# A quarter's y in three parts: dense products and the next quarter's kernel of lags traced between them

## The chip, the cores and the metric

One core of a Trainium2 chip runs the whole kernel. The metric is the device time of one execution in microseconds (us), the median of several runs. TensorE is PE in the profile, VectorE DVE, ScalarE ACT, GpSimd POOL, and SP is the queue that issues most DMAs.

## The reference, cut to what matters

One layer of a hybrid encoder over 1024 frames of 1024 channels, in float32:

```
u = rmsnorm(h);  proj = u @ w_in            # u_ssm | q | k | v
y_ssm  = S5 state space model(u_ssm)        # x_t = A x_{t-1} + B u_t ; y = Re(C x) + D u ; gelu ; GLU
y_attn = stick-breaking attention(q, k, v)  # 8 heads of 64
g_ssm, g_attn = sigmoid(u @ w_gate + b)
h = h + (g_ssm * (y_ssm @ w_up_ssm) + g_attn * (y_attn @ w_up_attn)) @ w_out
h = h + relu(rmsnorm(h) @ W1)^2 @ W2 ;  out = rmsnorm(h)
```

The change is in the part that forms y and its gelu in the state space model, and in how products of `u @ w_in` and `u @ w_gate` lie between its pieces.

## The kernel before, in words

The frames are cut into 128 blocks of 8. The states at the blocks' borders come from a tree of prefix sums on VectorE (`prefix_sums`). Then `ssm_y(q)` (L677) forms y for a quarter of the channels, q = 0 to 3, in three steps:

1. The kernel of lags: two loads on SP (L679: `cst[q]` to tag "h", `xq[q]` to tag "t"), a second "t" tile `tq`, eight 128x128 matmuls L686 into two "tr" banks of PSUM, and two copies L688 on ScalarE into `tq`.
2. y itself: the matmuls L700 to L702 into two "tr" banks (from `x`, `tq`, the states and `c`), two copies L703 into an "e" tile, and the gelu as a chain of four: square L705 on ScalarE, L706 on VectorE (in the trace under its helper's line, L145), sigmoid L707 on ScalarE, product L708 on VectorE (L142, e<-e,q).
3. The turn: eight transposes L714 into two "tr" banks, two copies L715 into a tile of tag "a", and its store to DRAM (L716, issued by SP at L76).

Each matmul of 128x128 float32 is two records in the trace, so L686 has 16 a quarter and L700, L701 and L702 have 16 each.

Beside this runs `fill`, a generator over the dense products (the projections of q, k, v and the gates, in pairs of weight blocks, seven products to a pair). An item has operands and a product. The operands (L604) are at most two sums, then a copy L620 on ScalarE to the high part and a subtraction L621 on POOL (in the trace L142, a<-a,a or a<-raw,a) to the low part, both in a new "a" tile. The product (L624) is 12 matmuls of 128x512 (L149, L152, L155) into one of the two "mm" banks. `pipelined(..., 2)` traces the operands of an item two items ahead of its product. The loop at L729 traces all of `ssm_y(q)` and then four steps of `fill` (BESIDE_Y), four times. After it comes the attention: its first steps turn v (L757, "tr" banks) and form scores (L779), and its weights go to "e" tiles in memory that the "e" and "four" tiles of this stage gave up (L835).

The order in which each engine runs its instructions isn't written by hand. It is fixed when the program is built: what is traced earlier goes first among what a timing model there holds to be ready. Tiles of a tag are given out in the order of tracing; a tile that is not free yet makes its first writer wait. The tags that matter: "tr" has 2 banks, "mm" 2, "t" 2 tiles, "a" 24 (of which the split activations `uT` hold 16 and their differences 2).

Of the kernel before, what the change touches and what calls it, by code (L numbers as in the profile page):

```python
# [31 lines left out]
BESIDE_Y = 4  # L32
# [21 lines left out]
def layer_kernel(ctx: ExitStack, tc: tile.TileContext, a, out):  # L54
# [17 lines left out]
    def stored(x, queue):  # L72

        count[0] += 1
        d = dp.tile([P, 1024], F32, tag=f"dram{count[0]}", name=f"dram{count[0]}")
        queue.dma_start(d, x)  # L76
        return d

    def load(src, tag):
        x = slot(tag)  # L80
        nc.sync.dma_start(x, src)
        return x

    def slot(tag, dtype=F32, cols=1024):
        count[0] += 1
        pool, bufs = beside.get(tag) or (sb, SLOTS[tag])
        return pool.tile([P, cols], dtype, tag=tag, bufs=bufs, name=f"{tag}{count[0]}")
# [11 lines left out]
    def bank(tag, dtype=F32):  # L99
        count[0] += 1  # L100
        return pp.tile([P, 512], dtype, tag=tag, bufs=BANKS[tag], name=f"{tag}{count[0]}")
# [39 lines left out]
    def tt(o, x, y, op, eng=None):  # L141
        (eng or V).tensor_tensor(o, x, y, op=op)  # L142

    def stt(o, x, s, y, op0, op1):
        V.scalar_tensor_tensor(o, x, s, y, op0=op0, op1=op1)  # L145
# [170 lines left out]
    with tc.issue_after(last_norm[0].ins):  # L316
# [19 lines left out]
        def exp_parts(x):  # L336

            xc = small()
            ts(xc, x, -88.0, ALU.max, 89.0, ALU.min)
            n = rounded(xc, 1.4426950408889634)  # L340
            r = small()
            stt(r, n, -0.693359375, xc, ALU.mult, ALU.add)
            stt(r, n, 2.12194440054690583e-4, r, ALU.mult, ALU.add)
            e = horner(r, [1.0 / math.factorial(i) for i in range(1, 10)])
            ni = small()
            nv = ni.bitcast(I32)
            ts(n, n, 127.0, ALU.add, 0.0, ALU.max)
            ts(n, n, 8388608.0, ALU.mult)
            V.tensor_copy(nv, n)
            pw = ni  # L350
            ex, em = small(), small()
            stt(ex, e, 1.0, pw, ALU.add, ALU.mult)
            tt(em, e, pw, ALU.mult)
            ts(r, pw, -1.0, ALU.add)
            tt(em, em, r, ALU.add)
            return ex, em

        dt, _ = exp_parts(ldt)
# [223 lines left out]
    def pipelined(items, ahead):  # L582

        for i in range(len(items) + ahead):
            if i < len(items):
                items[i][0]()
            if i >= ahead:
                items[i - ahead][1]()
                yield
# [87 lines left out]
    def ssm_y(q):  # L677

        c, x, tq = load(cst[q], "h"), load(xq[q], "t"), slot("t")  # L679

        tv = tq.rearrange("p (g t c) -> p t g c", g=8, t=L)
        for tb in range(2):
            ps = bank("tr")
            for i in range(4):
                t = tb * 4 + i
                PE.matmul(ps[:, i * P:(i + 1) * P], lhsT=iflat[:, (7 - t) * 16:(7 - t) * 16 + P],  # L686
                          rhs=kc[:, 512 + q * P:512 + (q + 1) * P], start=True, stop=True)
            S.activation(tv[:, tb * 4:tb * 4 + 4], ps.rearrange("p (t g c) -> p t g c", t=4, g=8), AF.Copy)  # L688
        y = slot("e")
        yv = y.rearrange("p (t g c) -> p g t c", t=L, g=8)  # L690
        tv = tq.rearrange("p (g x) -> p g x", g=8)
        cv = c.rearrange("p (g r x) -> p g r x", g=4, r=2)
        sv = sq[q]
        for e in range(2):
            ps = bank("tr")
            rows = slice(e * 64, e * 64 + 64)
            for i in range(4):
                g = 2 * i + e
                o = ps[:, i * P:(i + 1) * P]
                PE.matmul(o, lhsT=x[:, g * P:(g + 1) * P], rhs=tv[:, g], start=True, stop=False)  # L700
                PE.matmul(o, lhsT=sv[rows, 0, g // 2], rhs=cv[rows, g // 2, 0], start=False, stop=False)  # L701
                PE.matmul(o, lhsT=sv[rows, 1, g // 2], rhs=cv[rows, g // 2, 1], start=False, stop=True)  # L702
            S.activation(yv[:, e::2], ps.rearrange("p (g t c) -> p g t c", g=4, t=L), AF.Copy)  # L703
        w = slot("q")
        S.activation(w, y, AF.Square)  # L705
        stt(w, w, 1.0 / 0.044715, y, ALU.add, ALU.mult)  # L706
        S.activation(w, w, AF.Sigmoid, scale=2.0 * math.sqrt(2.0 / math.pi) * 0.044715)  # L707
        tt(y, y, w, ALU.mult)  # L708
        r = slot("a")
        rv = r.rearrange("p (k t) -> p t k", t=L)  # L710
        for th in range(2):
            ps = bank("tr")
            for i in range(4):
                PE.transpose(ps[:, i * P:(i + 1) * P], y[:, (th * 4 + i) * P:(th * 4 + i + 1) * P], ident)  # L714
            S.activation(rv[:, th * 4:th * 4 + 4], ps.rearrange("p (t k) -> p t k", t=4), AF.Copy)  # L715
        yT.append(stored(r, nc.sync))  # L716

    rest = [(j, p) for p in range(1, 4) for j in range(3)] + [("g", m) for m in GATES[PLAIN:]]
    fill = pipelined([x for i in range(0, len(rest), 2) for x in projected(rest[i:i + 2])], 2)
# [6 lines left out]
            next(sums, None)  # L726
    for _ in sums:
        pass
    for q in range(4):  # L729
        ssm_y(q)  # L730
        for _ in range(BESIDE_Y):
            next(fill)

    def split(x, tag):
# [625 lines left out]
```

## Time and profile before

| | us |
|---|---|
| median of 3 runs | 1528.75 |
| the three runs | 1527.75, 1528.75, 1528.93 |
| the profiled execution's own time | 1536.21 |
| its span, first to last instruction | 1534.1 |
| PE busy in the span | 1421.0 (93%) |
| mean granted clock of TensorE | 0.964 |

The profiled execution has its own time; around the span lie 2.11 us. A line of the timeline gives the start and the duration of an instruction or of a merged run of them (x10: ten), its engine and line, what it writes and reads, and in brackets how long the engine stood idle before it and what released it. [...]

### The profile page before, as it was taken

The numbers are of one execution on the slowest core, as the hardware profiler recorded it, in microseconds if no ns is written. First come the engines' busy times: TensorE is split into PE (matmuls) and PEld (weight loads), VectorE is DVE, ScalarE is ACT, GpSimd is POOL, SyncE is SP. The second block draws the span as 40 slices with busy tenths as digits, with TensorE's granted clock in tenths as the row PEclk, the third lists the DMA queues.
The fourth block names the chain that finished last, engine by engine and source line by source line (L and its number), as shares of the span: only waits on it lengthen the run. The fifth ranks groups of instructions, "written<-read, shape, count | busy, mean of one in ns | idle before, by whom it ended". The sixth has DMA issues, their size and how long they took to land.

```text
span 1534.1 us, 18436 instructions
## 1 busy us (share of the span) xinstructions
PE 1421.0 (93%) x6858; PEld 1123.2 (73%) x6858; DVE 1095.9 (71%) x1477; ACT 596.2 (39%) x1061; POOL 787.5 (51%) x448
## 2 busy tenths in 40 slices
PE   6999677998999899999999899999999899999786
PEld 6898556765666566678888678888887688887565
DVE  7996993128676767752734986655557999999997
ACT  5315112245555555641332633333332533333324
POOL 4102663134443333421240557777777788887963
PEclk9999799899999999999999999999999899999988
DMA  6113113232221211445421033333327433331002
GB/s 227 70 43 136 55 56 124 69 124 82 71 81 69 83 42 69 157 140 176 164 77 55 1 123 116 118 110 110 110 83 280 149 111 113 114 99 55 0 28 110
DMA packets 43432, 153.53 MB, mean 100 GB/s; under 512 B 5072, under 2 KB 5072, under 8 KB 43344
## 3 DMA queue, kind: packets, MB, share of 16 engines
q1 hardware_dynamic: 38448, 135.31, 26.1%
q10 hardware_dynamic: 4896, 17.06, 2.8%
q8 instruction: 54, 0.88, 0.2%
q14 instruction: 34, 0.28, 0.1%
HBM read 108.83 MB, written 43.52 MB: 99 GB/s over the span
## 4 chain that ended last, share of the span: by engine, by line
PE 36%; DVE 21%; issue 2%; POOL 1%; ACT 1%; DMA 1%; DVEq 0%; POOLq 0%; ACTq 0%
DVE a L142 5%; PE z L155 5%; PE z L152 5%; PE z L149 5%; DVE w L1149 5%; PE mm L149 4%; PE mm L152 4%; PE mm L155 3%; DVE h L142 3%; DVE raw L142 3%; PE tr L155 2%; PE tr L149 2%; PE tr L152 2%; DVE e L142 1%; DVE t L142 1%
## 5 line engine op out<-in xcount | busy, mean ns | idle before, releaser
L142 POOL TENSOR_TENSOR a<-raw,a 128x512 fp32r<-128x512 f32 (+2 forms) x70 | 99.1, 1424 | 245.3 <-ACT a L620 200.8
L149 PE MATMUL mm<-a,a 128*128 128x512 f32 (+1 forms) x369 | 147.0, 401 | 9.1 <-DVE a L142 6.9
L155 PE MATMUL mm<-a,a 128*128 128x512 f32 (+1 forms) x369 | 143.2, 389 | 1.9 <-DVE a L142 1.8
L152 PE MATMUL mm<-a,a 128*128 128x512 f32 (+1 forms) x369 | 144.4, 392 | 0.0
L790 DVE TENSOR_TENSOR_SCAN e<-e 128x512 f32<-128x512 f32 (+3 forms) x96 | 111.8, 1174 | 44.2 <-ACT e L785 44.1
L142 POOL TENSOR_TENSOR a<-a,a 128x512 fp32r<-128x512 f32 x36 | 53.3, 1481 | 122.4 <-ACT a L620 122.1
L142 POOL TENSOR_TENSOR a<-e,a 128x512 fp32r<-128x512 f32 (+1 forms) x71 | 107.8, 1530 | 10.7 <-ACT a L1038 9.8
L1038 ACT ACTIVATE a<-e 128x512 fp32r<-128x512 f32 x84 | 52.6, 631 | 137.9 <-POOL e L142 37.1
L142 DVE TENSOR_TENSOR a<-mm,a 128x512 f32<-128x512 f32 x96 | 65.2, 681 | 57.2 <-PE mm L155 52.8
L149 PEld LDWEIGHTS mm<-a,a 128*128 128x128 f32 x369 | 71.5, 195 | 25.0 <-issue 8.1
L155 PEld LDWEIGHTS mm<-a,a 128*128 128x128 f32 x369 | 71.3, 193 | 16.8 <-DVE a L142 2.2
L152 PEld LDWEIGHTS mm<-a,a 128*128 128x128 f32 x369 | 71.8, 195 | 13.3 <-DVE a L257 0.3
L142 DVE TENSOR_TENSOR a<-a,a 128x512 f32<-128x512 f32 (+2 forms) x52 | 58.6, 1131 | 30.5 <-ACT a L620 10.3
L132 POOL TENSOR_TENSOR w<-raw,w 128x1024 fp32r<-128x1024 f32 x13 | 33.3, 2564 | 82.3 <-ACT w L131 82.3
L1149 POOL TENSOR_TENSOR e<-a,e 128x1024 fp32r<-128x1024 f32 (+1 forms) x24 | 73.8, 3079 | 2.7 <-ACT e L1148 2.7
L1149 POOL TENSOR_TENSOR e<-raw,e 128x1024 fp32r<-128x1024 f32 x21 | 56.0, 2669 | 25.9 <-ACT e L1148 25.9
L152 PE MATMUL z<-e,w 128*128 128x512 f32 x156 | 63.3, 406 | 6.0 <-POOL e L1149 6.0
L155 PE MATMUL mm<-w,a 128*128 128x512 f32 x158 | 67.3, 426 | 0.0
L152 PE MATMUL mm<-w,a 128*128 128x512 f32 x158 | 67.2, 425 | 0.0
L142 DVE TENSOR_TENSOR e<-e,e 128x256 f32<-128x256 f32 (+4 forms) x81 | 62.7, 784 | 4.9
L149 PE MATMUL mm<-w,a 128*128 128x512 f32 x158 | 65.7, 416 | 0.0
L149 PE MATMUL z<-e,w 128*128 128x512 f32 x156 | 62.6, 402 | 3.0 <-DVE q L142 3.0
(543 smaller groups left out, 4313.1 us busy)
## 6 DMA issues: line engine op xcount, KB each, us to landing
a<-dram SPq DMA_DIRECT2D x36, 512.0 KB, 3.6
dram<-a SPq DMA_DIRECT2D x32, 512.0 KB, 2.6
dram<-q ACTq DMA_DIRECT2D x30, 512.0 KB, 2.6
a<-wff SPq DMA_DIRECT2D x30, 512.0 KB, 4.3
q<-dram SPq DMA_DIRECT2D x20, 512.0 KB, 3.3
raw<-wff SPq DMA_DIRECT2D x18, 512.0 KB, 3.6
raw<-wgate SPq DMA_DIRECT2D x16, 512.0 KB, 3.6
e<-wff SPq DMA_DIRECT2D x15, 512.0 KB, 3.6
```

The costliest lines, as they stand in the source:

```text
L132: G.tensor_tensor(lo, raw, f32(hi), op=ALU.subtract)
L142: (eng or V).tensor_tensor(o, x, y, op=op)
L149: PE.matmul(ps, lhsT=lh[0], rhs=rh[0], start=first, stop=False)
L152: PE.matmul(ps, lhsT=lh[0], rhs=rh[1], start=False, stop=False)
L155: PE.matmul(ps, lhsT=lh[1], rhs=rh[0], start=False, stop=last)
L790: V.tensor_tensor_scan(fr, fr, fr, 1.0 if last else f[:, hi:hi + 1], op0=ALU.mult, op1=ALU.bypass)
L1038: S.activation(w[:, lh], x, AF.Copy)
L1149: eng.tensor_tensor(lo, x, f32(hi), op=ALU.subtract)
```

## The change

`ssm_y` becomes a generator that stops after the kernel of lags, after the gelu, and after the turn. The loop traces the first kernel of lags ahead, and then for each quarter: y and gelu, one step of `fill`, the next quarter's kernel of lags, one step of `fill`, the turn, and the last two steps of `fill`. No instruction is added or removed.

```diff
@@ ssm_y, after the copies L688
+        yield
         y = slot("e")
...
@@ after the gelu, L708
         tt(y, y, w, ALU.mult)
+        yield
         r = slot("a")
...
@@ after the store L716
         yT.append(stored(r, nc.sync))
+        yield
...
@@ the loop, L729
+    quarters = [ssm_y(q) for q in range(4)]
+    next(quarters[0])
     for q in range(4):
-        ssm_y(q)
-        for _ in range(BESIDE_Y):
+        next(quarters[q])
+        next(fill)
+        if q < 3:
+            next(quarters[q + 1])
+        next(fill)
+        next(quarters[q])
+        for _ in range(BESIDE_Y - 2):
             next(fill)
```

## Rows read from the trace of the kernel before

**Rows 1.** Windows from one quarter's first L700 to the next's, the last to 342.5.

```profile
239.89:266.52 26.63, 23.70 (x124) 18.32 (x122) 5.37 (x7) 8.88 (x13) 8.79 (x7) 1.00 0.33 119
266.52:298.35 31.83, 30.52 (x129) 23.42 (x130) 5.80 (x7) 9.10 (x13) 7.18 (x6) 0.79 0.20 66
298.35:323.01 24.66, 23.19 (x121) 17.96 (x121) 4.36 (x6) 8.98 (x13) 10.33 (x8) 1.00 0.30 107
323.01:342.50 19.49, 17.52 (x93) 13.20 (x93) 4.42 (x4) 8.36 (x12) 2.58 (x3) 1.00 0.36 119
```

**Rows 2.** Timeline of PE, from the end of quarter 0's y.

```profile
248.24 0.50 PE L155 MATMUL mm<-h,a 128*128 128x512 f32 x1
...
253.82 1.09 PE L714 MATMUL tr<-iext,e 128*128 128x128 f32 x8 [0.31 <-DVE e L142]
255.71 1.42 PE L686 MATMUL tr<-h,iext 128*128 128x128 f32 x10 [0.80 <-ACT a L715]
...
258.42 0.50 PE L155 MATMUL mm<-h,a 128*128 128x512 f32 x1 [0.62 <-POOL a L142]
...
266.52 0.49 PE L700 MATMUL tr<-t,t 128*128 128x128 f32 x2 [1.20 <-ACT t L688]
```

**Rows 3.** Timeline of ACT, quarter 0's gelu and turn.

```profile
248.98 1.06 ACT L705 ACTIVATE q<-e 128x1024 f32<-128x1024 f32 x1
...
254.57 2.02 ACT L715 ACTIVATE a<-tr 128x512 f32<-128x512 f32 x2 [2.18 <-PE tr L714]
256.37 1.68 ACT L620 ACTIVATE a<-raw 128x512 fp32r<-128x512 f32 x3
```

**Rows 4.** Timeline of PE, the low clock of quarter 1 and its end.

```profile
279.57 0.79 PE L152 MATMUL mm<-a,a 128*128 128x512 f32 x1
...
282.96 0.39 PE L149 MATMUL mm<-a,a 128*128 128x512 f32 x1
```

**Rows 5.** Timeline of PE, quarter 2: y, dense products, turn.

```profile
298.35 0.40 PE L700 MATMUL tr<-t,t 128*128 128x128 f32 x2
...
306.72 0.50 PE L152 MATMUL mm<-a,a 128*128 128x512 f32 x1
...
311.20 0.39 PE L155 MATMUL mm<-q,a 128*128 128x512 f32 x1
312.19 1.09 PE L714 MATMUL tr<-iext,e 128*128 128x128 f32 x8 [0.60 <-DVE e L142]
314.02 1.42 PE L686 MATMUL tr<-h,iext 128*128 128x128 f32 x10 [0.74 <-ACT a L715]
```

**Rows 6.** Timeline of SP, loads and stores beside quarters 0 and 1.

```profile
231.09 0.33 SPq L81 DMA_DIRECT2D raw<-wqkv  x1
...
234.34 13.69 SPq L81 DMA_DIRECT2D t<-dram  x2
```

**Rows 7.** ACT by shapes, 235 to 342: line, xcount, busy and mean ns.

```profile
L715 ACT ACTIVATE a<-tr 128x512 f32<-128x512 f32 x8 | 8.1, 1115 | 7.5 <-PE tr L714 7.5
L620 ACT ACTIVATE a<-a 128x512 fp32r<-128x512 f32 x8 | 4.8, 629 | 10.0 <-POOL a L142 6.3 <-DMA dram<-a 3.6
...
L688 ACT ACTIVATE t<-tr 128x512 f32<-128x512 f32 x8 | 4.6, 593 | 7.8 <-DVE four L142 4.3 <-PE tr L686 3.4
```

**Rows 8.** Timeline of DVE, a subtraction beside one of POOL, and one alone.

```profile
295.50 0.69 DVE L142 TENSOR_TENSOR a<-a,a 128x512 fp32r<-128x512 f32 x1 [0.58 <-ACT a L620]
...
340.53 1.37 DVE L142 TENSOR_TENSOR a<-a,a 128x512 fp32r<-128x512 f32 x1 [3.14 <-ACT a L620]
```

**Rows 9.** Timeline of POOL, the subtraction beside that one.

```profile
340.06 1.29 POOL L142 TENSOR_TENSOR a<-a,a 128x512 fp32r<-128x512 f32 x1 [15.68 <-ACT a L620]
```

**Rows 10.** Windows, the attention's first 25 us.

```profile
340.00:365.00 25.00, 21.09 (x98) 14.06 (x96) 20.88 (x21) 13.08 (x30) 12.68 (x9) 0.86 0.35 126
```

**Rows 11.** Timeline of PE, one of the later falls of the clock, first and last.

```profile
352.94 0.77 PE L149 MATMUL mm<-h,a 128*128 128x512 f32 x1
...
357.78 0.42 PE L155 MATMUL mm<-q,a 128*128 128x512 f32 x1
```

## The prediction

> **What bounds the kernel now.** I read the windows first, one from each quarter's first y matmul to the next's. In the first three PE is busy for all but 26.63 − 23.70 = 2.93, 31.83 − 30.52 = 1.31 and 24.66 − 23.19 = 1.47 us, while DVE, ACT and POOL are each busy for under half [rows 1]. So PE is the bound here, and two things can be won: its idle time, together 5.71 us, and its clock, which stands at 0.79 in the second quarter and 1.00 in the others.
>
> Then the timeline of PE shows where the idle time lies. In quarter 0 it is four gaps: 0.31 before the turn, waiting for the gelu; 0.80 before the next kernel of lags, which wants a "tr" bank that L715 is still copying out; 0.62 in a dense product that waits for POOL's low part; 1.20 before quarter 1's y, which waits for L688 [rows 2]. Their sum is the 2.93 of the window. Quarter 2 repeats the pattern, 0.60 and 0.74 [rows 5].
>
> Third, ACT's timeline tells why PE has nothing else to do. Between the end of y at 248.24 and the turn at 253.82 [rows 2] PE can run only the two products whose operands were traced before `ssm_y`. The next three copies L620 start at 256.37, right behind the start of L715 [rows 3], although ACT stood idle for 2.18 us before L715 and the raw block of the two later ones had been asked for at 231.09 [rows 6]. I read this as the order in which "a" tiles are given out: the turn's tile `r` is traced before those operands, so their tiles wait until L715, its first writer, has its place. Then L715 takes ACT for 2.02 us, POOL follows, and the product comes late. That is an inference from times; no row names it.
>
> **The change, part by part.** Nothing is added or removed; costs come from order alone.
>
> *Two steps of `fill` ahead of the turn.* Their operands are now traced before `r`, so the copies can run under y's matmuls, when ACT and POOL have room. PE gets four products in place of two to lie around the turn. A product costs 2.8 us: 20 matmuls from 306.72 to 311.20 are 19 steps of 0.236, times 12 [rows 5].
>
> *The gelu's cover.* From the end of y to the turn the chain takes 5.58 us (248.24 to 253.82) [rows 2]. The moved kernel of lags puts two copies L688 of 0.593 us [rows 7] onto ACT; between square and sigmoid they would make the chain 6.77 us. Cover is two products, 5.66, and the kernel of lags, 16 records that I take at the 1.42 us of ten plus six more at the same rate, 2.3 [rows 2]: 7.9 us. The wait for the gelu goes, if the fixed order puts the turn late enough.
>
> *The kernel of lags between.* It now takes the "tr" banks that y gave up instead of those of the turn, so the 0.80 and the 0.74 behind L715 go. The turn in its place needs the banks back from L688; those copies are done within the chain above. L715's 2 × 1.115 us [rows 7] now stand before the next y's banks, under two products of 5.66 us. And L688 is long done when the next y starts, so the 1.20 goes. Queued behind a late turn on PE would be two products and the next y.
>
> *The loads that move with it.* `c` and `x` of the next quarter are now traced ahead of the turn's store and of the later raw blocks. SP is in order and already stands 13.69 us at such a load, waiting for the "t" tiles that y is reading [rows 6]. The same wait comes, at the same event; what is behind it are a store and raw blocks, wanted two products later. I cost it at nothing, hidden by those products; without them it would be at most the 1.20 that quarter 1's y waited.
>
> *The last quarter* has no kernel of lags. Its window holds 19.49 − 17.52 = 1.97 us of idle time [rows 1], but behind it stands the attention's start, where DVE is busy for 20.88 of 25 us [rows 10] and waits for this turn, not for PE. Bounds 0 to 1.97; I take 0, since the turn itself comes after the same chain.
>
> *The clock.* Quarter 1's y takes 279.57 − 266.52 = 13.05 us [rows 2, 4], quarter 2's 306.72 − 298.35 = 8.37 [rows 5]: 4.68 lost. The next eight matmuls take 282.96 − 279.57 = 3.39 [rows 4] where 8 × 0.236 is 1.89: 1.50 more. Before that fall PE had stood idle 0.62 and 1.20 [rows 2]; the quarters with no gap in front of y kept 1.00 [rows 1]. With dense products right up to y I expect 1.00 in all four: 6.18 us. Bounds 0, if the fall isn't there in the runs without a profile, to 6.18. [...]
>
> *What stays.* PE's order is fixed beforehand and the chip's times differ, so I keep one wait a quarter at the largest of its kind, 0.74 [rows 5]: 3 × 0.74 = 2.22; bounds 0 to all of 5.71. One thing speaks for a price: operands that now run beside the gelu put POOL's subtractions beside DVE's. A DVE subtraction took 1.37 us beside one of POOL's and 0.69 alone [rows 8, 9], so the gelu's two steps on DVE could take 2 × 0.68 = 1.36 us longer: 8.1 us in the chain with the copies against 7.9 of cover, a wait of 0.2, which the 0.74 holds. [...]
>
> **Sum.** 5.71 + 6.18 − 2.22 = 9.67 us. All durations are of the profiled execution, 1536.21 us with a span of 1534.1; the median of the plain runs is 7.46 lower. Taken off the median: 1528.75 − 9.67 = 1519.1. PE's work is the same, so time won here moves everything behind it, and I book nothing further down, where falls of the clock will land elsewhere: one, from 352.94 to 357.78, costs 4.84 − 11 × 0.236 = 2.2 us [rows 11].
>
> **The rivals.** *The fall of the clock isn't in the plain runs.* The three lie within 1.18 us, so they all have it or none has; that the profiled one is 7.46 slower speaks for none, that the program's order and so the gap in front are the same in every run speaks for all. Then 1528.75 − 5.71 + 2.22 = 1525.3.
>
> *Nothing happens.* PE's order is set by what the model holds ready, not by tracing alone; where the old order already had the next kernel of lags as early as its banks let it, and where later stages take back what is won, the time stays 1528.75. Against it: the banks and tiles are given out by tracing, and that is what changes.
>
> *"a" tiles run out: slower.* Six of the 24 are left to `fill` and `r`. Around the turn of quarter 1 two results, one sum and four operands want seven, and `r` comes behind them. ACT has already waited 3.6 us for a store to free such a tile [rows 7]. If every turn waits so, beyond what the products in front of it cover, the stage pays up to 4 × 3.6 = 14.4 us: 1519.1 + 14.4 = 1533.5. It decides from a wait of 9.67 / 4 = 2.4 us a turn. Against it: each product that ends frees a tile, and two end before each turn.
>
> **How the numbers follow.** My forecast gets 0.44. The clock's absence gets 0.26, the unchanged time 0.16, the missing tiles 0.14. A measurement of this kernel can tell about 0.2% from no change, 3.06 us, so faster means under 1525.7. The forecast is all faster. 1525.3 lies just under the bound: 0.16 of its 0.26 faster, 0.10 same. The unchanged case is 0.14 same and 0.02 slower, the missing tiles slower. Together 0.60, 0.24, 0.16. The low end is all idle time gone, the last quarter's too: 1528.75 − 5.71 − 1.97 − 6.18 = 1514.9, and 0.9 for falls of the clock further down, 1514.0. The high end takes in the unchanged case with the 1.2 between the runs, 1530.0, and leaves the missing tiles out. The likeliest case alone spans 1514.9 to 1522.6, where the 5.71 stays whole.
>
> **What would show it.** In the changed profile the next quarter's L686 stands between two products before L714; copies L620 run while y's matmuls run; gaps before L686 and L700 are gone; the distance from one y to the next is about 23.5 us in place of 26.63, 31.83 and 24.66; the granted clock is 1.00 in all four windows; the attention's first scan on DVE comes about 10 us earlier. Wrong would be: L714 idle for over 2 us behind the gelu or L715 waiting for a store (tiles), a fall of the clock in another y, or the stage shorter by 10 us and the end not (taken back in the attention).

## The result and the profile after

The changed kernel takes 1517.1 us (median of 4 runs, 1516.05 to 1519.29) against 1528.76 for the kernel before (4 runs). The ratio is 0.9917 with a 95% interval of [0.9888, 0.9946]: 11.7 us faster, where 9.7 were forecast (1519.1). The profiled execution has its own time of 1516.05 us, with a span of 1514.0.

First the page of the profile after, the lines of PE and of the granted clock:

```profile
PE 1410.6 (93%) x6858; PEld 1118.9 (74%) x6858; DVE 1095.6 (72%) x1477; ACT 597.3 (39%) x1061; POOL 787.6 (52%) x448
...
PEclk9999889999999999999999999999999999999999
```

No instruction was added or removed, yet PE is busy for 10.4 us less than the 1421.0 of before. Most of it is the clock, since busy time counts a slow matmul at its slow length (L149 takes 0.63 us at 280.58 in the slow stretch of before, 0.39 at 282.96): a second profile of the kernel before, without that stretch (below), has PE busy for 1414.6, 6.4 us less, of which quarter 1's window has 30.52 − 24.46 = 6.06.

The windows after, again from one quarter's first y matmul to the next's, the last from quarter 3's y on:

```profile
240.94:262.57 21.63, 21.63 (x119) 17.76 (x118) 5.46 (x7) 7.71 (x11) 6.41 (x5) 1.00 0.36 134
262.57:284.64 22.07, 22.07 (x121) 18.14 (x120) 4.76 (x5) 10.28 (x16) 7.22 (x7) 1.00 0.29 102
284.64:306.72 22.08, 22.08 (x122) 18.14 (x121) 5.33 (x6) 9.09 (x13) 10.82 (x9) 1.00 0.33 119
306.72:325.00 18.28, 18.24 (x96) 14.42 (x95) 4.62 (x6) 7.88 (x11) 3.92 (x4) 1.00 0.27 91
```

These answer to [rows 1]. Span and busy time of PE are the same number in the first three: PE doesn't stand for a moment from quarter 0's y to quarter 3's, and the clock is 1.00, full speed on the scale of the page, throughout. Three quarters take 65.78 us in place of 83.12.

PE's timeline of quarter 0 answers to [rows 2]. The y matmuls are now L701 to L703, the turn is L716:

```profile
249.28 0.50 PE L155 MATMUL mm<-h,a 128*128 128x512 f32 x1
...
251.68 1.95 PE L686 MATMUL tr<-h,iext 128*128 128x128 f32 x16
...
256.23 1.03 PE L716 MATMUL tr<-iext,e 128*128 128x128 f32 x8
...
262.57 0.38 PE L701 MATMUL tr<-t,t 128*128 128x128 f32 x2
```

No bracket is left: not before the kernel of lags, not before the turn, not before the next y. The kernel of lags is one run of 16 records, no longer cut in two (10 in [rows 2], the other 6 behind two products). The order is the one forecast: the rest of one product, lags, a product, the turn, two products, y.

ACT's timeline shows why the products are there:

```profile
237.31 0.63 ACT L620 ACTIVATE a<-raw 128x512 fp32r<-128x512 f32 x1
240.67 0.63 ACT L620 ACTIVATE a<-raw 128x512 fp32r<-128x512 f32 x1 [2.73 <-PE mm L155]
...
250.02 1.06 ACT L706 ACTIVATE q<-e 128x1024 f32<-128x1024 f32 x1
252.37 1.06 ACT L708 ACTIVATE q<-q 128x1024 f32<-128x1024 f32 x1 [1.29 <-DVE q L145]
253.34 1.07 ACT L688 ACTIVATE t<-tr 128x512 f32<-128x512 f32 x2
256.86 2.18 ACT L717 ACTIVATE a<-tr 128x512 f32<-128x512 f32 x2 [2.46 <-PE tr L716]
```

Two copies L620 run at 237.31 and 240.67, the first ahead of quarter 0's y and the second as it begins, so even earlier than the forecast had them; in [rows 3] the same kind of copy came only behind the turn's copies, at 256.37. The two copies L688 run behind the sigmoid and don't lengthen the gelu.

### The profile page after: what moved, and what is told of

Same layout as the page of the kernel before. It is cut to its first block, busy times and chain, and to the rows that moved or that the text cites. A ratio compares the mean times of both kernels' runs of the same rounds, so it can differ in the third digit from the quotient of the medians.

```text
span 1514.0 us, 18438 instructions
## 1 busy us (share of the span) xinstructions
PE 1410.6 (93%) x6858; PEld 1118.9 (74%) x6858; DVE 1095.6 (72%) x1477; ACT 597.3 (39%) x1061; POOL 787.6 (52%) x448
## 4 chain that ended last, share of the span: by engine, by line
PE 35%; DVE 21%; issue 2%; POOL 1%; ACT 1%; DMA 1%; DVEq 0%; POOLq 0%; ACTq 0%
DVE a L142 6%; PE z L155 5%; PE z L152 5%; PE z L149 5%; DVE w L1160 5%; PE mm L149 4%; PE mm L152 4%; PE mm L155 4%; DVE h L142 3%; DVE raw L142 3%; PE tr L149 2%; PE tr L155 2%; PE tr L152 2%; DVE e L142 1%; DVE t L142 1%
## 5 line engine op out<-in xcount | busy, mean ns | idle before, releaser
L149 PE MATMUL mm<-a,a 128*128 128x512 f32 (+1 forms) x369 | 148.5, 405 | 13.2 <-DVE a L142 11.8
L149 PEld LDWEIGHTS mm<-a,a 128*128 128x128 f32 x369 | 71.9, 196 | 28.8 <-issue 12.0
L149 PE MATMUL z<-e,w 128*128 128x512 f32 x156 | 63.1, 404 | 3.0 <-DVE q L142 3.0
L149 PE MATMUL mm<-w,a 128*128 128x512 f32 x158 | 64.8, 410 | 0.0
```

The lines of the kernel that those rows point to most:

```text
L149: PE.matmul(ps, lhsT=lh[0], rhs=rh[0], start=first, stop=False)
```

## The experiments

Three questions were left. Is it the turn's tile `r` that kept the dense operands back (theory A), or the two "tr" banks (rival B)? Is the slow clock of quarter 1's y, called the fall below, in the median of the kernel before? And does it depend on how few dense matmuls stand ahead of y (theory C)? Ten experiments ran. Each was timed beside the kernel before on the same chip, and a ratio is to that.

**The kernel before again**, unchanged.

> The kernel before, unchanged, to see whether the fall of the clock in quarter 1's y (13.05 us instead of 8.37, mean granted clock 0.964 over a span of 1534.1) belongs to every execution. If it does, the profile taken here has a quarter of about 31.8 us again and a clock of 0.964, and the time around 1528.8 already holds it. If it is only in some, the profile here shows that quarter at about 25.5 us, a clock of 0.967 or more, and a span near 1526.6, which is the median less the 2.1 us that lie around the span.

Measured: 1531.11 us (10 runs, 1528.47 to 1537.19), the kernel before beside it 1531.28 (21 runs); ratio 0.9999 [0.9975, 1.0024]. The profile taken here has no fall in y:

```profile
241.10:267.41 26.31, 23.67 (x123) 18.29 (x121) 5.35 (x7) 8.90 (x13) 8.79 (x7) 1.00 0.33 121
267.41:293.18 25.77, 24.46 (x130) 18.91 (x130) 5.81 (x7) 9.12 (x13) 7.20 (x6) 1.00 0.25 83
293.18:317.85 24.67, 23.17 (x121) 17.96 (x121) 4.36 (x6) 9.01 (x13) 10.39 (x8) 1.00 0.28 106
```

The second quarter takes 25.77 us here and took 31.83 in the profile on which the prediction rests [rows 1], with the same program. Over all three series of the kernel before (53 executions with a clock), 19 take 1533.9 to 1537.3 us at a mean clock of 0.964 to 0.967, and 34 take 1525.5 to 1532.0 at 0.969 to 0.974, with nothing between. The first profile is of the smaller group, and the four runs behind the 1528.76 are of the larger. So the fall, as far as times and clocks tell it, belongs to about a third of the executions and not to that median. (One profile of each group was taken, the first with the fall and this one without; that the others of a group are like them is inferred.)

**The kernel of lags alone** is moved between y and the turn; all four dense steps stay behind the turn. The edit is shown against the changed kernel.

```diff
     for q in range(4):
         next(quarters[q])
-        next(fill)
         if q < 3:
             next(quarters[q + 1])
-        next(fill)
         next(quarters[q])
-        for _ in range(BESIDE_Y - 2):
+        for _ in range(BESIDE_Y):
             next(fill)
```

> Half of the change: the next quarter's kernel of lags is traced between y and the turn, all four dense steps stay behind the turn. Theory A (the turn's tile r, traced ahead of the dense operands, keeps them back): the waits behind L715 and L688 go (0.80, 0.74 and 1.20 of the idle time), but behind each turn PE stands about 1.5 to 2 us for a product whose operands come only after L715 and POOL; 1524 to 1528. Rival B (the two tr banks are what holds PE back): nearly the whole gain is here, 1516 to 1520.

Measured: 1525.39 us (10 runs), ratio 0.9954 [0.9933, 0.9974]. PE's timeline behind the first turn, then ACT's:

```profile
254.09 1.03 PE L716 MATMUL tr<-iext,e 128*128 128x128 f32 x8
...
257.40 0.50 PE L149 MATMUL mm<-h,a 128*128 128x512 f32 x1 [0.90 <-ACT a L620]
...
258.76 0.50 PE L155 MATMUL mm<-h,a 128*128 128x512 f32 x1 [0.63 <-POOL a L142]
```

```profile
254.78 2.14 ACT L717 ACTIVATE a<-tr 128x512 f32<-128x512 f32 x2 [2.11 <-PE tr L716]
256.69 1.68 ACT L620 ACTIVATE a<-raw 128x512 fp32r<-128x512 f32 x3
```

The waits for a bank and for L688 are gone, as both said. But three copies L620 stand behind the turn's copies exactly as in [rows 3], and PE waits 0.90 + 0.63 us for them. That is A's picture; about half of the gain is missing.

**The dense steps alone** are moved ahead of the turn; the kernel of lags stays right ahead of its y. The edit is again against the changed kernel.

```diff
     for q in range(4):
         next(quarters[q])
-        next(fill)
-        if q < 3:
-            next(quarters[q + 1])
-        next(fill)
+        for _ in range(2):
+            next(fill)
         next(quarters[q])
         for _ in range(BESIDE_Y - 2):
             next(fill)
+        if q < 3:
+            next(quarters[q + 1])
```

> The other half: two dense steps are traced between y and the turn, the next quarter's kernel of lags stays behind the last dense step of the quarter, just ahead of its y. Theory A: PE has four products around the turn, the waits for the gelu and for POOL go, only a wait for L688 of up to 1.2 us can stay ahead of each next y; 1517 to 1521. Rival B: the banks hold PE as before; 1525 to 1529.

Measured: 1519.04 us (6 runs), ratio 0.9915 [0.9884, 0.9945]. Nearly the whole gain comes with the dense steps, as A said, and B's 1525 to 1529 is out. Its profile happens to hold a fall, one of two in six runs (1523.67 and 1524.54). PE's timeline from the kernel of lags to quarter 1's y, and the first matmul behind it:

```profile
262.61 0.48 PE L149 MATMUL mm<-a,a 128*128 128x512 f32 x1
262.93 0.39 PE L152 MATMUL mm<-a,a 128*128 128x512 f32 x1
263.16 0.39 PE L155 MATMUL mm<-a,a 128*128 128x512 f32 x1
263.39 0.40 PE L149 MATMUL mm<-a,a 128*128 128x512 f32 x1
264.16 0.49 PE L701 MATMUL tr<-t,t 128*128 128x128 f32 x2 [0.37 <-ACT t L688]
...
267.33 0.79 PE L701 MATMUL tr<-t,t 128*128 128x128 f32 x2
...
276.69 0.79 PE L152 MATMUL mm<-a,a 128*128 128x512 f32 x1
```

Ahead of this y stand the kernel of lags, four dense matmuls and an idle 0.37 us. From 267.33 on the pairs L701 take 0.79 us in place of 0.49, and the dense matmul behind y is still slow. This y took 276.69 − 264.16 = 12.53 us. On ACT two copies L620 run at 237.89 and 240.83, as in the changed kernel.

**The turn's tile of another tag**, in the order of tracing of the kernel before.

```diff
-        r = slot("a")
+        r = slot("q")
         rv = r.rearrange("p (k t) -> p t k", t=L)
```

> The order of tracing of the kernel before, only the turn's tile r is of tag q instead of a. Theory A, that tiles of a tag are given out in the order of tracing and r therefore holds back the operands traced after it: the dense products come free without any move, and the time is that of the run with the dense steps alone, within 1.5 us. Rivals (the banks, or the order of tracing itself as a priority): as before, 1527 to 1530.

Measured: 1515.22 us (4 runs), ratio 0.9879 [0.984, 0.9918], and no line of the loop was moved. ACT's timeline:

```profile
237.55 0.63 ACT L620 ACTIVATE a<-raw 128x512 fp32r<-128x512 f32 x1
240.90 0.63 ACT L620 ACTIVATE a<-raw 128x512 fp32r<-128x512 f32 x1 [2.71 <-PE mm L155]
245.39 0.60 ACT L703 ACTIVATE e<-tr 128x512 f32<-128x512 f32 x1 [3.86 <-PE tr L702]
...
256.55 2.21 ACT L715 ACTIVATE q<-tr 128x512 f32<-128x512 f32 x2 [2.86 <-PE tr L714]
```

The copies L620 are traced behind the turn and still run 16 us and more ahead of its copies, since they no longer share a tag with `r`. This shows the inference of the prediction: what held the dense products back was one tile of a shared tag, given out in the order of tracing. That it is the order, and not only that tag "a" has a tile more here, follows from the dense steps alone: there `r` is still of tag "a" and the copies run as early. The time was expected within 1.5 us of the dense steps alone; it is 3.8 below them.

**A second series**: the changed kernel, the changed kernel with `r` of tag q, and two kernels of above, side by side; the kernel before beside them took 1529.16 us (11 runs).

> The changed kernel once more, beside the three others of this call on one chip. Theory C (the clock falls in a quarter's y only where few dense matmuls stand ahead of it, as in the kernel before and in the run with the dense steps alone, where the kernel of lags and four dense matmuls stand there): no execution here has the long quarter, the runs lie within 4 us of each other, 1515 to 1520. Rival (the fall is chance in every order): some executions are 5 to 8 us slower than the others at a clock 0.005 lower, as 12 of 31 of the kernel before were.

> The changed kernel with the turn's tile r of tag q. Theory A: the operands are free of r already in the changed order, so nothing is left to win in the stage (three quarters of about 22.1 us); 1514 to 1519, within 1.5 us of the changed kernel unless the attention's order differs. If the tag of r by itself is what made that run reach 1515.2 (one a tile more for the dense products), it is 2 to 4 us faster than the changed kernel.

> The kernel before with r of tag q, again. Its PE order in the stage is that of the run with the dense steps alone: kernel of lags and four dense matmuls right ahead of y. Theory C: some of its executions have the fall in a y and are 5 to 8 us slower (the run with the dense steps alone had 2 of 6), so its median over more runs rises to 1515 to 1518. Rival (luck has no part): 1515 with a spread under 4 us.

> The dense steps alone again, for the share of executions with the fall: theory C expects a third of them at 1523 to 1525 and the others at 1518 to 1519; the fast ones then lie within 1.5 us of the changed kernel, so that moving the kernel of lags is worth little but the absence of the fall.

| | median us | runs | lowest to highest | ratio |
|---|---|---|---|---|
| changed | 1516.56 | 6 | 1514.72 to 1517.5 | 0.9911 [0.9888, 0.9933] |
| changed, `r` of tag q | 1513.31 | 5 | 1512.05 to 1513.68 | 0.9888 [0.9864, 0.9912] |
| before, `r` of tag q | 1514.73 | 6 | 1513.93 to 1518.68 | 0.9903 [0.9877, 0.9928] |
| dense steps alone | 1519.93 | 6 | 1516.22 to 1523.3 | 0.9935 [0.9909, 0.996] |

The changed kernel has no long execution in ten. The dense steps alone have two more (1523.16 at a clock of 0.966, 1523.3 at 0.964), four in twelve; the median of their other eight is 1518.4, against 1516.9 for the ten of the changed kernel. But theory C falls in its strict form: the kernel before with `r` of tag q has the same order of PE in the stage as the dense steps alone, lags and four dense matmuls right ahead of y, and none of its ten executions has a clock under 0.969. One thing sets it apart: in its profile of this series PE doesn't stand ahead of quarter 1's y (at 262.86, without a bracket), while in the two profiles with a fall it stands there for 1.20 [rows 2] and 0.37 us. That stop does not decide alone either, since profiles of the same two kernels have the stop and no fall. First the kernel before again, then the dense steps alone again, where this y takes 8.45 us:

```profile
267.41 0.49 PE L700 MATMUL tr<-t,t 128*128 128x128 f32 x2 [0.92 <-ACT t L688]
```

```profile
264.35 0.49 PE L701 MATMUL tr<-t,t 128*128 128x128 f32 x2 [0.37 <-ACT t L688]
...
272.80 0.50 PE L152 MATMUL mm<-a,a 128*128 128x512 f32 x1
```

What decides on the fall is left open. The kernel of lags alone, which has no stop there, has two executions at a clock of 0.966 (1528.67 and 1528.96), and no profile tells what they hold.

The changed kernel with `r` of tag q beats both kernels of this study: its slowest execution is faster than the changed kernel's fastest of this series. Its three quarters are no shorter (65.78 us again), so the 3 us lie behind them. One guess was the order at the attention's start, where it runs the first scores ahead of v's turn.

**The first scores traced ahead of v's turn**, in the changed kernel and in the one with `r` of tag q.

```diff
     head_in(0)
-    converted(0)
+    heads[0] = coming_in[0]
     ws = []
     for _ in weights(0, 0, ws):
         pass
+    converted(0)
```

> The changed kernel, only that the attention's first scores are traced ahead of v's first turn (L768). If the 3 us by which the kernel with r of tag q beat it (1513.3 against 1516.6) come from the attention's start, where that kernel ran the first scores ahead of v's turn and DVE's first scans came earlier: 1513 to 1515. If they come from the tile that the tag a gained: 1516 to 1517.5.

> Both: r of tag q and the first scores traced first. If the attention's start is the cause, the order there is nearly what it was with r of tag q alone, so 1512.5 to 1514, nothing added. If tile and order are two causes: 1509 to 1511.

Measured: 1517.67 us (6 runs), ratio 0.9906 [0.9881, 0.9931], and 1512.88 us (6 runs), ratio 0.9872 [0.9847, 0.9896]. Tracing the scores first brings nothing; the tag brings its gain again, 4.8 us between these two medians. The order itself was reproduced only in part: traced so, PE runs v's turn at 327.56, behind the first block's scores alone, where with `r` of tag q it comes at 330.30, behind the second block's too. Two of the six runs of the first kernel stand 3 us above its others (1520.92 and 1521.3, at 0.969), and no profile of them was taken. The waits of PE from 325 to 460 us, each with its total, count and longest, first for the changed kernel in the second series, then with `r` of tag q, then with the scores first:

```profile
PE tr L817 <- DVE e L142: 3.0, 3, 1.3
```

```profile
PE tr L817 <- DVE e L142: 2.0, 2, 1.3
...
PE tr L768 <- DMA q<-dram: 0.8, 1, 0.8
```

```profile
PE tr L817 <- DVE e L142: 4.8, 4, 2.2
```

PE waits less for DVE at the attention's start with the tag, 2.0 us in place of 3.0 and 4.8, and once for a load instead. A second thing differs there, the clock. The same three profiles from 325 to 345 us:

```profile
325.00:345.00 20.00, 18.82 (x87) 11.99 (x86) 14.00 (x19) 10.74 (x26) 10.31 (x8) 0.83 0.40 148
```

```profile
325.00:345.00 20.00, 19.20 (x106) 12.20 (x106) 16.38 (x21) 12.12 (x29) 9.01 (x7) 1.00 0.57 198
```

```profile
325.00:345.00 20.00, 17.15 (x87) 11.11 (x86) 15.62 (x19) 10.60 (x26) 9.86 (x8) 0.83 0.42 147
```

From quarter 3's y to the attention's first product with v (L833) the changed kernel takes 340.09 − 306.47 = 33.62 us and the one with the tag 337.09 − 306.78 = 30.31. The 3.3 between them are about the whole gain, and the 12 dense matmuls just ahead of L833 are 0.93 of it: 3.88 us with the first of them at the lower clock (L149 takes 0.63 at 337.63 and 0.39 at 338.63), 2.95 with all at 1.00. So the gain is in part less waiting and in part a fall of the clock that doesn't come. Why it doesn't, and whether the "a" tile that the dense products gain or v's later load, which now waits for `r`'s tile, is behind both, isn't told apart.

## Why the prediction was right, and where it was not

The direction and the mechanism by which the idle time goes were right. Of the three terms of the sum two were not, and what they had wrong, together with gains that the sum left out, nearly cancelled; that the forecast came within 2 us of the time is luck in that part. The fair comparison is of two profiles without a fall, the kernel before again and the changed kernel again, up to the first copy behind the attention (L736 before, L747 after):

```profile
L736 ACT ACTIVATE a<-a x4: 1042/1049/1061, 633.0 to 638.5; 128x1024 fp32r<-128x1024 f32 x4
```

```profile
L747 ACT ACTIVATE a<-a x4: 1040/1047/1063, 618.4 to 623.9; 128x1024 fp32r<-128x1024 f32 x4
```

```profile
240.69:262.32 21.63, 21.63 (x119) 17.77 (x118) 5.46 (x7) 7.71 (x11) 6.40 (x5) 1.00 0.38 140
262.32:284.40 22.08, 22.08 (x122) 18.14 (x121) 4.76 (x5) 10.29 (x16) 7.21 (x7) 1.00 0.30 102
284.40:306.47 22.07, 22.07 (x122) 18.14 (x120) 5.33 (x6) 9.09 (x13) 10.82 (x9) 1.00 0.34 120
```

By L747 the changed kernel is 633.0 − 618.4 = 14.6 us ahead: 0.38 at the first y (241.07 against 240.69; the window shown above begins 0.03 late), 76.78 − 65.78 = 11.00 in three quarters, 3.22 from there on. Behind it the spans lose 0.9 again.

- *The idle time, 5.71:* right. The kernel before again stands for 5.34 us in these windows by the same brackets, the changed one for none. The reading that a tile of the turn holds the operands back, marked as an inference, is shown by the run with `r` of tag q.
- *What stays, −2.22:* wrong, nothing stays. (The 0.74 wasn't the largest wait of its kind either: [rows 2] has 0.80.) The gelu is done at 253.58 + 1.22 = 254.80 and the turn starts at 256.23. The extra length of DVE's steps beside POOL came once and small, 1.46 us in place of 1.22 for the gelu's product in quarter 1, and it was covered:

```profile
275.64 1.46 DVE L142 TENSOR_TENSOR e<-e,q 128x1024 f32<-128x1024 f32 x1 [0.98 <-ACT q L708]
```

```profile
274.74 1.28 POOL L142 TENSOR_TENSOR a<-a,a 128x512 fp32r<-128x512 f32 x1 [6.16 <-ACT a L620]
```

  The prediction took the 0.68 of [rows 8, 9] as the price of each of the gelu's two steps on DVE. But POOL had started first both times, and when DVE's step started, only 341.35 − 340.53 = 0.82 us of POOL's were left there, and 276.02 − 275.64 = 0.38 here; DVE took 0.68 and 0.24 longer, each 0.14 less than what was left. So the 0.68 is no fixed price of a step beside POOL; what sets the price, these two cases don't show.
- *The clock, 6.18:* this is the step that failed as a term of the sum. The size was right for an execution that has the fall, but the sum was taken off a median of runs that had none. The first rival said just this and got 0.26; its condition holds. The argument against it, that the same order must bring the same fall in every run, does not: one program with one order took 31.83 us for that quarter in one profile and 25.77 in the other. The rival's time, 1525.3, was 8 us too high for the reasons above and below this point. What makes the clock fall in one execution and not in the next no run shows; the 19 of 53 executions are taken as those with the fall.
- *What the sum left out:* a stop costs more than its bracket. Summed from start to start and without the brackets, the 48 records of the kernel of lags went from 5.82 to 5.12 us, the three turns from 3.12 to 2.37, and the dense matmuls from 35.83 (146 of them) to 33.25 (142), of which the four fewer are 0.92. That is 0.70 + 0.75 + 1.66 = 3.1 us of matmuls that hold PE longer beside a wait or after a change of kind. In the kernel before the dense matmul at 258.42, behind the wait of 0.62 [rows 2], has the next one 0.34 us behind it (258.76), and so has the one at 257.07, right behind the kernel of lags (257.41); the one at 252.89 has it 0.23 behind (253.12), and that one, the last ahead of the wait for the gelu, stands for its whole 0.39. The rest of the 11.00 are 1.49 us of first scores that ran ahead of quarter 1's turn, the four matmuls, and 0.14 in y; the scores and the matmuls come later now and aren't won.
- *The last quarter, 0:* too low. PE's idle time there went up to 325 us (18.28 against 18.24 busy), and with the attention 3.22 us were won though more work lay there; how much of them is the clock further down isn't told apart. DVE's first scan came 342.81 − 329.21 = 13.6 us earlier by the two first profiles, while quarter 3's y came 16.3 earlier: two products now run ahead of v's turn, which costs the scan 2.7 us of it. By the two profiles without a fall it came 337.66 − 328.96 = 8.7 us earlier, where about 10 were forecast.
- *"Nothing happens"* and *"a" tiles run out:* neither. The tiles were indeed what mattered, but the change freed them; no L717 waits for a store. Two copies L620 wait for one, 1.03 us at 283.85 and 1.32 at 326.67, both under dense work.

## What to carry to other kernels

Where a builder gives out tiles of a shared tag in the order of tracing, a late result traced early holds back every later tile of that tag; look for an engine that stands idle ahead of a copy whose input has long been there, and either trace the independent work first or give the late result a tag of its own. The one-line change of tag won as much here as the reordering (1514.73 us against 1516.56 in the second series). Before a slow stretch of the clock in one profile goes into a sum, look whether the plain runs have it: their clocks (here 0.964 to 0.967 in the 19 long executions, 0.969 to 0.974 in the others), or their spread, tell.

## What the runs showed that was not expected

The same program has two times, 1525.5 to 1532.0 and 1533.9 to 1537.3 us, and of the two profiles that were taken the one of the longer group has a fall of the clock within one quarter's y: 8.37 us of small matmuls at the high level become 13.05, though PE never stops in them (no bracket from 266.94 to 279.57), and the clock comes back only with the dense matmuls behind them (0.63 us at 281.87, 0.39 at 282.96). The changed kernel, with dense products right up to y, had no such execution in ten, a gain that its median against the quick executions of before doesn't show: against the long ones it is 1536.44 − 1516.56 = 19.88 us, by the median of the 19 and that of the second series. That dense products ahead of y are what keeps the clock up is not shown; the kernel before with `r` of tag q has only four of them there and had no such execution in ten either.
